# First stage in nine uneven parts, first feed-forward products from unnormalized rows, low-rank products split in two halves of precision, and a new hand-made order

## The chip, the core and the metric

The kernel runs on one core of one Trainium2 chip, as one program with one launch. The metric is the device time of an execution in microseconds (us); less is better. The kernel before has a median of 2166.08 us over three executions (2161.04, 2166.35 and 2166.08). The execution that was profiled took 2172.5 us.

## What is computed

One layer over 256 latent tokens and 256 context tokens of width 2048, all in float32. Cut to what matters here:

```python
mod = silu(c) @ w_ada + b_ada                     # six rows of 2048: shift, scale, gate, twice
h  = modulate(rmsnorm(x, n1), sh1, sc1)           # latent tokens
hc = modulate(rmsnorm(ctx, n1), csh1, csc1)       # context tokens, rows of their own
p  = h @ w_in ; pc = hc @ w_in                    # RWKV r,k,v + low-rank columns, GDN q,k,v, z, gates
# RWKV-7, 16 heads of 64, both directions: decay and in-context rate come from low-rank products,
#   tanh(wd) @ w2 and ad @ a2 (rank 96, two directions each); gate = sigmoid(gd) @ g2
# gated DeltaNet, 8 heads of 128, in chunks, both directions
# final states of the context scans start the latent scans
y  = (sigmoid(g_a) * (o_a @ p_a) + sigmoid(g_b) * (o_b @ p_b)) @ w_out
x  = x + gt1 * y
z  = modulate(rmsnorm(x, n2), sh2, sc2)           # (x * r) * s2 + sh2 with one factor r per token
x  = x + gt2 * (silu(z @ w_gate) * (z @ w_up)) @ w_down
return rmsnorm(x, nf)
```

## The kernel before

**Matrices.** Activations lie with the 2048 channels on 16 tiles of 128 partitions and the tokens on the free axis. Every large product is made in three passes of a faster float32 format (`fp32r`): each operand is cast to a high half `hi` (ScalarE, `whi`) and its remainder `lo` is formed (VectorE, `wlo`), and `gemm` adds hi·hi, hi·lo and lo·hi for each of the 16 tiles of the contraction. A weight tile of 128 columns comes in two pieces of 512 KB over SyncE's DMA queue (`load_w`, or `cast` in the middle stage).

**First stage** (`p0`, lines 440 to 565). x and ctx are loaded, their squares summed, and then eight parts follow, each for two of the 16 channel tiles: four loads of 1 MB of `ada_first`, 64 small TensorE products with it (`ada_part`, line 494), a copy and a transpose (`rows_of`, lines 500 and 502) that make shift and scale, the normalized rows `hxh` and `hxl` (lines 513 to 516), the split of two rows of `w_low` (line 527), and the products of 736 columns that all the rest waits for (`low_products`, through `gemm`, lines 399 to 401): the low-rank columns and the first pair's k and r, in six accumulators. The products of a part stand between the small products of the next one, in amounts that `TILES` sets. At the end two DMAs clear the scratch `tscr` in DRAM from a zero tile of 130 columns.

**Middle stage** (from line 820 on). RWKV pairs, DeltaNet heads, the remaining columns of `w_in` (`products`) and 64 rows of `ada_rest` are written as generators. `Weave` puts their instructions in one order on every engine: it keeps a modelled clock per engine, and picks what could begin first, with `RANK` for ties. This order is what runs (all its instructions show line 147). Tiles of gate columns (`g`), which nothing in this stage needs, fill TensorE; `GATES_A` and `GATES_B` say after which pair or head how many of the 40 become eligible. Products for k, v, K and V cover latent and context tokens at once (512 columns), those for r, Q and g the latent ones (256). The 32 low-rank products (`lowrank`, rank 96) are plain float32.

**After it.** `rows`, the RWKV result, is split into `oah` and `oal` (lines 404 and 405), then come 16 tiles with `p_a`, 16 with `p_b`, 16 with `w_out`. The gate columns are read back (`gate_rows`) into `gts`, which takes the place of `hxh` and `hxl`. During these the last two blocks of `ada_rest` (`scale2`, line 1656) are summed on VectorE, which gives shift and scale of the feed-forward part, and the weights of its first four tiles (`W4`) are loaded and split. Then `rms_scale` (line 418) makes the factor r per token, 16 tiles of `hfh` and `hfl` follow (lines 1753 to 1755), and the first four feed-forward tiles run over them, channel tile by channel tile.

Of the kernel before, what the change touches and what calls it, by code (L numbers as in the profile page):

```python
# [11 lines left out]
F32 = mybir.dt.float32  # L12
# [6 lines left out]
P = 128  # L19
D = 2048  # L20
KT = D // P
# [6 lines left out]
GATES_A, GATES_B = (5, 3, 2, 1, 0, 1, 5, 3), (3, 1, 0, 0, 2, 2, 9, 3)  # L28

RANK = dict(cast=-99, lowrank=194, prepare=47, grams=45, inverse=-73, values=-11, scan=-101, begin=184, head_scan=142, head_inverse=129, head_grams=55, decays=83, outputs=126, head_solve=187, tokens=12, features=125, gate_out=97, lowrank_out=104, row_tile=523)  # L30
# [273 lines left out]
def emit(ctx: ExitStack, tc, A, out, dbg=None):  # L304
# [61 lines left out]
    zero = cst.tile([P, 130], F32, name="zero")  # L366
    G.memset(zero, 0.0)
# [43 lines left out]
    H2 = (hx.tile([P, KT, 2, T], F32R, name="hxh"), hx.tile([P, KT, 2, T], F32R, name="hxl"))  # L411
    HX = tuple(t.rearrange("p k a t -> p k (a t)") for t in H2)
# [27 lines left out]
    NE = 8  # L440
    with tc.tile_pool(name="p0", bufs=1) as p0, \
# [12 lines left out]
        def load_ada(e, c):  # L454
            w = aws[e, c] = p0.tile([P, 4, 4, P], F32, tag="aw", name="aw", bufs=6)
            Q.dma_start(w, A["ada_first"][e, :, 4 * c:4 * c + 4])

        def load_low(e):
            lws[e] = [wp.tile([P, 8, P], F32, tag="wraw", name="wraw", bufs=3).rearrange("p k m -> p (k m)")[:, :NL]
                      for _ in range(2)]  # L460
            for k in range(2):
                Q.dma_start(lws[e][k], A["w_low"][e, :, k])
# [26 lines left out]
        def ada_part(ps, e, c):  # L489

            for i in range(4):
                k = 4 * c + i
                for g in range(4):
                    E.matmul(ps[32 * g:32 * g + 32, 0:P], ckr[:, k].rearrange("p a b -> p (a b)"), aws[e, c][:, i, g],
                             start=k == 0, stop=k == KT - 1)

        def rows_of(e, ps, between):
# [7 lines left out]
            pv = pt[:, 0:P].rearrange("p (a k i) -> p a k i", a=2, k=2)  # L505
            g = slice(2 * e, 2 * e + 2)
            for i, m in enumerate((mod, modc)):
                V.tensor_add(m[:, 0:32].rearrange("p (a k) -> p a k", a=2)[:, :, g], pv[:, :, :, 16 * i],
                             p_("bada")[:, 0:32].rearrange("p (a k) -> p a k", a=2)[:, :, g])
                V.scalar_tensor_tensor(s1[:, i, g], m[:, 16 + 2 * e:18 + 2 * e], 1.0, p_("n1")[:, g], ALU.add, ALU.mult)  # L510
            todo = [(src, i, k, m) for k in range(2 * e, 2 * e + 2) for i, (src, m) in enumerate(((xt, mod), (ct, modc)))]
            for src, i, k, m in todo:
                V.scalar_tensor_tensor(src[:, k, :], src[:, k, :], s1[:, i, k:k + 1], rs[:, i], ALU.mult, ALU.mult)
                S.activation(H2[0][:, k, i, :], src[:, k, :], AF.Identity, bias=m[:, k:k + 1])
            for src, i, k, m in todo:
                V.scalar_tensor_tensor(H2[1][:, k, i, :], src[:, k, :], m[:, k:k + 1], H2[0][:, k, i, :].bitcast(F32),
                                       ALU.add, ALU.subtract)

        def low_split(e):
            res = []  # L520
            for k in range(2):
# [42 lines left out]
        for t in tscr:  # L564
            Q.dma_start(t.rearrange("(p a n) -> p a n", p=P, a=8), zero.unsqueeze(1).to_broadcast([P, 8, 130]))
# [197 lines left out]
    def lowrank():  # L763

        yield s.preload_act_table_set(SIGM)
        lin = rs.tile([P, 2, 8, 2, 64], F32, tag="KBx", name="lin", bufs=2).rearrange("p a b c d -> p (a b c d)")[:96].rearrange("p (j t) -> p j t", j=4)
        raw = rs.tile([P, 4, 64], F32, tag="Y", name="raw").rearrange("p a b -> p (a b)")[:64]
        ab = rs.tile([P, 512], F32, tag="iv0", name="ab")[:32]
        for j, b in ((0, pib), (2, psb), (1, mmb), (3, psb)):
            ps = low[j]  # L770
            yield from shift(ps, 96, 24 + j, lin[:, j])
            if j < 2:
                yield s.activation(lin[:, j], lin[:, j], AF.Tanh)
# [4 lines left out]
            weave.release(b)  # L778
        out = [rs.tile([P, 8, 2, 64], F32, tag=f"VX{i}", name="lo").rearrange("p a b c -> p (a b c)") for i in range(2)]
        out = [t[:, n:n + 512] for t in out for n in (0, 512)]  # L780
        for p in range(NPAIR):
            if p == 2:
# [7 lines left out]
                yield s.activation(sgd, sgd, AF.Exp, scale=-1.0)  # L790
            if p % 2 == 0:
                w = wp.tile([P, 8, P], F32, tag="wraw", name="wraw", bufs=3)
                yield dq(w[:96], A["lora"][p // 2])
            for j in (0, 2, 1, 3):
                ps = yield psb
                yield e.matmul(ps, w[:96, 4 * (p % 2) + j], lin[:, j], start=True, stop=True)
                weave.add(RANK['lowrank_out'], lowrank_out(p, j, ps, out[j]))
# [79 lines left out]
    def grams(p, d):  # L877
# [8 lines left out]
        if d == 0:  # L886
# [33 lines left out]
        p2m, KB, KBx = o["p2m"], o["KB"], o["KBx"]  # L920
# [984 lines left out]
```

## Time and profile before

| what | value |
|---|---|
| median of three executions | 2166.08 us |
| profiled execution: its time, its span | 2172.5 us, 2170.7 us |
| mean granted TensorE clock | 0.988 of full |
| TensorE busy | 2099.3 us, 97% of the span, 24140 matmuls |
| weight loads on TensorE (beside the matmuls) | 1904.9 us, 88% |
| VectorE busy | 1484.0 us, 68% |
| ScalarE busy | 1120.4 us, 52% |
| GpSimd busy | 76.2 us, 4% |
| DMA | 435 MB, 200 GB/s on the mean, 418 GB/s from 25 to 100 us |

PE stands for TensorE's matmuls, PEld for its weight loads, DVE for VectorE, ACT for ScalarE, POOL for GpSimd, SP for SyncE. A row of the timeline gives the start and duration in us, engine, line, operation, output tile, input tiles, shape and count, and in brackets how long the engine was idle before and what it then waited for. A row of the stretches gives for each engine the busy time and the number of instructions, then the granted TensorE clock (PEclk, 1.00 is full), the share of the DMA engines' time and GB/s. Matmuls are pipelined: a duration contains the drain, so the rate is read from one start to the next. A float32 matmul shows as two records.

### The profile page before, as it was taken

Reading aid. Unit: us, or ns where it says so; the run is one execution under the profiler, and the core shown is the slowest. Engines: PE = TensorE matmul, PEld = TensorE weight load, DVE = VectorE, ACT = ScalarE, POOL = GpSimd, SP = SyncE. Lnnn points to the kernel's source line nnn. Section 1 sums busy time; section 2 is a strip of 40 time slices with the busy share of each in tenths; the row PEclk is TensorE's granted clock in tenths of the full one; section 3 lists DMA queues with packets and bytes.
Section 4 is the critical chain, followed back from the end, with each engine's and each line's share of the span. In section 5 each row is a group of like instructions: output and inputs, shape, how many; then the busy total and the mean of one; then the engine's idle time right before and its main releaser. Section 6 shows DMA issues by size and latency. Waiting matters only on the chain.

```text
span 2170.7 us, 56983 instructions
## 1 busy us (share of the span) xinstructions
PE 2099.3 (97%) x24140; PEld 1904.9 (88%) x24140; DVE 1484.0 (68%) x2974; ACT 1120.4 (52%) x2126; POOL 76.2 (4%) x169
## 2 busy tenths in 40 slices
PE   6999999999999999999999999999999999999997
PEld 4777787788888788878988999999999999999997
DVE  4456798888877687898887589856565665444454
ACT  3249853564555666566744555444444444444443
POOL 0000000000000010000010001000000000000000
PEclk9999999999999999999999999999999999999999
DMA  9967544343543364466686899837777775566665
GB/s 387 418 175 204 179 125 116 102 122 102 135 130 103 119 230 131 133 200 186 207 280 216 271 331 342 300 101 234 235 235 231 231 233 192 188 180 186 187 187 156
DMA packets 235278, 435.17 MB, mean 200 GB/s; under 512 B 115216, under 2 KB 130576, under 8 KB 230544
## 3 DMA queue, kind: packets, MB, share of 16 engines
q1 hardware_dynamic: 207376, 356.03, 52.1%
q0 software_dynamic: 13824, 50.34, 7.0%
q10 hardware_dynamic: 13824, 25.17, 3.6%
q8 instruction: 189, 3.10, 0.6%
q14 instruction: 65, 0.53, 0.1%
HBM read 405.63 MB, written 25.84 MB: 199 GB/s over the span
## 4 chain that ended last, share of the span: by engine, by line
issue 51%; PE 9%; DMA 4%; DVE 3%; ACT 1%; POOL 1%; SPq 0%; POOLq 0%; DVEq 0%; ACTq 0%
PE mm L147 6%; DMA aw<-ada_rest 4%; PE pa L147 1%; PE s L147 1%; DVE wlo L147 1%; DVE aw L147 1%; DVE arena L147 1%; PE pi L147 1%; DMA inX<-tscr 0%; POOL aw L1654 0%; DVE inX L147 0%; DMA tscr<-arena 0%; ACT whi L147 0%; POOL aw L125 0%; ACT arena L147 0%
## 5 line engine op out<-in xcount | busy, mean ns | idle before, releaser
L390 DVE TENSOR_TENSOR wlo<-wraw,whi 128x1024 fp32r<-128x1024 f32 x328 | 392.6, 1198 | 325.0 <-ACT whi L389 322.5
L389 ACT CAST whi<-wraw 128x1024 fp32r<-128x1024 f32 x328 | 337.4, 1030 | 464.5 <-PE mm L400 414.6
L147 PE MATMUL mm<-hxh,wlo 128*128 128x256 f32 (+1 forms) x1376 | 463.5, 337 | 7.4 <-DVE wlo L147 7.2
L147 PE MATMUL mm<-hxh,whi 128*128 128x256 f32 (+1 forms) x1376 | 463.2, 337 | 1.7 <-DVE arena L147 1.7
L147 PE MATMUL mm<-hxl,whi 128*128 128x256 f32 (+1 forms) x1376 | 463.4, 337 | 0.6 <-issue 0.6
L400 PE MATMUL mm<-hfl,whi 128*128 128x256 f32 x1344 | 377.3, 281 | 0.0
L401 PE MATMUL mm<-hfh,wlo 128*128 128x256 f32 x1344 | 376.5, 280 | 0.0
L399 PE MATMUL mm<-hfh,whi 128*128 128x256 f32 x1344 | 374.1, 278 | 0.0
L147 PEld LDWEIGHTS mm<-hxh,wlo 128*128 128x128 f32 x1376 | 262.9, 191 | 36.8 <-DVE wlo L147 12.0
L147 DVE TENSOR_TENSOR wlo<-wraw,whi 128x512 fp32r<-128x512 f32 x344 | 234.9, 686 | 79.0 <-ACT whi L147 76.9
L147 PEld LDWEIGHTS mm<-hxh,whi 128*128 128x128 f32 x1376 | 263.1, 191 | 25.2 <-issue 3.1
L147 PEld LDWEIGHTS mm<-hxl,whi 128*128 128x128 f32 x1376 | 263.2, 191 | 25.0 <-issue 4.8
L401 PEld LDWEIGHTS mm<-hfh,wlo 128*128 128x128 f32 x1344 | 252.7, 188 | 0.2
L399 PEld LDWEIGHTS mm<-hfh,whi 128*128 128x128 f32 x1344 | 252.8, 188 | 0.0
L400 PEld LDWEIGHTS mm<-hfl,whi 128*128 128x128 f32 x1344 | 252.4, 188 | 0.0
L147 ACT CAST whi<-wraw 128x512 fp32r<-128x512 f32 x344 | 205.7, 618 | 89.4 <-PE mm L147 74.1
L399 PE MATMUL mm<-za,whi 128*128 128x256 f32 x512 | 143.9, 281 | 0.0
L401 PE MATMUL mm<-za,wlo 128*128 128x256 f32 x512 | 143.8, 281 | 0.0
L400 PE MATMUL mm<-za,whi 128*128 128x256 f32 x512 | 143.7, 281 | 0.0
L401 PEld LDWEIGHTS mm<-za,wlo 128*128 128x128 f32 x512 | 96.6, 189 | 0.0
L399 PEld LDWEIGHTS mm<-za,whi 128*128 128x128 f32 x512 | 96.5, 189 | 0.0
L400 PEld LDWEIGHTS mm<-za,whi 128*128 128x128 f32 x512 | 96.5, 189 | 0.0
(360 smaller groups left out, 3860.6 us busy)
## 6 DMA issues: line engine op xcount, KB each, us to landing
wraw<-w SPq DMA_DIRECT2D x172, 512.0 KB, 3.8
wraw<-wgu SPq DMA_DIRECT2D x168, 512.0 KB, 4.7
aw<-ada_rest POOLq DMA_DIRECT2D x96, 512.0 KB, 5.9
aw<-ada_first SPq DMA_DIRECT2D x32, 1024.0 KB, 13.6
wraw<-wdn SPq DMA_DIRECT2D x64, 448.0 KB, 3.6
wraw<-wout SPq DMA_DIRECT2D x32, 512.0 KB, 6.3
aw<-ada_gt ACTq DMA_DIRECT2D x64, 256.0 KB, 5.0
wraw<-wdn SPq DMA_DIRECT2D x32, 512.0 KB, 3.7
```

What stands on the lines that cost most here:

```text
L147: return Op(self, cost, lambda: getattr(self.engine, name)(out, *a, **k), kind)
L389: S.copy(hi[:, c, :M], raw[:, c, :M])
L390: V.tensor_sub(lo[:, c, :M], raw[:, c, :M], hi[:, c, :M].bitcast(F32))
L399: E.matmul(ps, hi, Xh[:, k, :n], start=first and i == 0, stop=False)
L400: E.matmul(ps, hi, Xl[:, k, :n], start=False, stop=False)
L401: E.matmul(ps, lo, Xh[:, k, :n], start=False, stop=last and i == len(wt) - 1)
```

## The change

**First stage.** Nine parts take the place of eight: one channel tile in the first and in the last, two in the seven between. `ada_first` is laid out for it; a part with one channel tile has two loads of 1 MB instead of four, and its shift and scale are added from two rows of the small products. `TILES` has ten entries. The scratch is no longer cleared here.

**Split tiles.** `hxh` and `hxl` become four tiles, high and low of the latent and of the context tokens (`h00` and so on). Each matmul over 512 columns becomes two over 256 (`parts`), in the order hi·hi latent, hi·hi context, hi·lo latent, hi·lo context, lo·hi latent, lo·hi context.

**Middle stage.** The scratch is cleared in the middle stage by a generator (`zeros`) that fills a tile of 1040 columns on GpSimd and copies it out in two DMAs. Each low-rank product becomes three `fp32r` products; their activations are split after the shift (`lin`), their weights in a generator of its own (`lowrank_weights`), each half of which waits until the previous pair's products have read it (`lowdone`). `RANK`, `GATES_A` and `GATES_B` have new values; several generators wait for one more event, since tiles are shared in another way. `merge_rows` also splits the RWKV result, once the context halves are free (`h01`).

**After it.** `PA` and the gate columns lie in the other three tiles. `scale2` advances by two steps in each of the first ten tiles of `w_out` and one in the eleventh; the four tiles of `W4` are loaded at tiles 10 to 13 and not at 1, 4, 7 and 10. The first four channel tiles of the first four feed-forward tiles are multiplied with x1·s2 without the factor r, together with two columns of the shift (258 columns), before and after `rms_scale`; the result is multiplied by r and added to that of the other twelve channel tiles, which are made as before.

```diff
-GATES_A, GATES_B = (5, 3, 2, 1, 0, 1, 5, 3), (3, 1, 0, 0, 2, 2, 9, 3)
-RANK = dict(cast=-99, lowrank=194, prepare=47, grams=45, inverse=-73, values=-11, scan=-101, begin=184, ...)
+GATES_A, GATES_B = (5, 4, 1, 2, 0, 2, 6, 3), (1, 2, 0, 0, 2, 3, 6, 3)
+RANK = dict(cast=-105, lowrank=22, prepare=69, grams=28, inverse=-48, values=38, scan=-6, begin=131, ...)
...
-    H2 = (hx.tile([P, KT, 2, T], F32R, name="hxh"), hx.tile([P, KT, 2, T], F32R, name="hxl"))
+    H2 = [[hx.tile([P, KT, T], F32R, tag=f"h{i}{j}", name=f"h{i}{j}") for j in range(2)] for i in range(2)]
+    def parts(ps, w, k, n, first, last):
+        hi, lo = w
+        todo = [(u, H2[i][j][:, k], j) for u, i in ((hi, 0), (hi, 1), (lo, 0)) for j in range(n // T)]
+        for i, (u, x, j) in enumerate(todo):
+            yield ps[:, T * j:T * j + T], u, x, first and i == 0, last and i == len(todo) - 1
...
-    NE = 8
+    PARTS = ((0, 1),) + tuple((k, 2) for k in range(1, 15, 2)) + ((15, 1),)
+    NE = len(PARTS)
...
-        TILES = ((0, 0), (2, 2), (2, 2), (2, 2), (1, 3), (2, 2), (1, 3), (1, 2), (2, 2))
+        TILES = ((0, 0), (3, 3), (2, 2), (2, 2), (1, 3), (2, 2), (1, 3), (1, 2), (2, 2), (2, 2))
...
-        for t in tscr:
-            Q.dma_start(t.rearrange("(p a n) -> p a n", p=P, a=8), zero.unsqueeze(1).to_broadcast([P, 8, 130]))
...
+            for i in range(2):
+                yield "lw", p, i
+                hi, lo = lw[i]
+                for j in (i, i + 2):
+                    ps = yield psb
+                    c = slice(P * (j // 2), P * (j // 2) + P)
+                    yield [e.matmul(ps, a[:, c], x, start=n == 0, stop=n == 2)
+                           for n, (a, x) in enumerate(((hi, lin[j][0]), (hi, lin[j][1]), (lo, lin[j][0])))]
+                weave.ready("lowdone", p, i)
...
-            for j in (0, 2, 1, 3):
-                ps = yield psb
-                yield e.matmul(ps, w[:96, 4 * (p % 2) + j], lin[:, j], start=True, stop=True)
+            for i in range(2):                        # lowrank_weights
+                if p:
+                    yield "lowdone", p - 1, i
+                own = w[:96, 4 * (p % 2) + i:4 * (p % 2) + i + 3:2]
+                hi, lo = (t.rearrange("p (j c) -> p j c", j=2) for t in lw[i])
+                yield v.tensor_copy(hi, own)
+                yield v.tensor_sub(lo, own, hi.bitcast(F32))
+                weave.ready("lw", p, i)
...
+        both = hx.tile([P, KT, T], F32R, tag="h01", name="oa")          # merge_rows
+        Oa.extend((both[:, 0:8], both[:, 8:16]))
+        for i in range(0, 8, 2):
+            yield s.copy(Oa[0][:, i:i + 2, :], rows[:, i:i + 2, :])
+            yield v.tensor_sub(Oa[1][:, i:i + 2, :], rows[:, i:i + 2, :], Oa[0][:, i:i + 2, :].bitcast(F32))
...
-        for _ in itertools.islice(scale_next, 2 if j in (0, 3, 6, 9, 12) else 1):
+        for _ in itertools.islice(scale_next, STEPS[j]):                # [2] * 10 + [1] + [0] * 5
...
+    pu = [pst(psq, "s"), pst(psq, "s"), pst(pi, "pi"), pst(pa, "pa")]
+    for a in range(4):
+        gemm(pu[a][:, 0:T + 2], w4[a][:NU], Xu, T + 2)                  # NU = 4
+        if not a:
+            r = rms_scale(x1p, [ssum, sq], T, "rs")
...
-        for k in range(KT):
+        for k in range(NU, KT):
             for a in range(4):
-                gemm(p4[a // 2][:, T * (a % 2):T * (a % 2) + T], w4[a][k:k + 1], Hf, T,
-                     k == 0 and a % 2 == 0, k == KT - 1 and a % 2 == 1)
+                     k == NU and a % 2 == 0, k == KT - 1 and a % 2 == 1)
+        for a in range(4):
+            tc.keep_in_program_order(V.tensor_copy(wsh[:, a:a + 1], pu[a][:, T:T + 1]))
+            tc.keep_in_program_order(V.tensor_mul(both[a // 2][:, T * (a % 2):T * (a % 2) + T], pu[a][:, 0:T], r))
+        for a in range(4):
+            o = slice(T * (a % 2), T * (a % 2) + T)
+            V.scalar_tensor_tensor(both[a // 2][:, o], both[a // 2][:, o], wsh[:, a:a + 1], p4[a // 2][:, o], ALU.add, ALU.add)
```

More of the change, by code (lines that the diff above doesn't have):

```diff
@@ L489, in ada_part @@
         def ada_part(ps, e, c):
[L491 to L495, printed above, removed]
+            n = PARTS[e][1]
+            if (e, c) not in aws:
+                return
+            w = aws[e, c]
+            for i in range(8 // n):
+                k = 8 // n * c + i
+                for a in range(2 * n):
+                    g = 2 * n * (i % (2 // n)) + a
+                    E.matmul(ps[32 * g:32 * g + 32, 0:P], ckr[:, k].rearrange("p a b -> p (a b)"), w[:, i, a],
+                             start=k < 2 // n, stop=k >= KT - 2 // n)
         def rows_of(e, ps, between):
@@ L520, in low_split @@
             res = []
-            for k in range(2):
+            for k in range(PARTS[e][1]):
                 pool = p0 if e % 2 else wp
@@ L770, in lowrank @@
             ps = low[j]
-            yield from shift(ps, 96, 24 + j, lin[:, j])
+            x = full[j % 3 > 0]
+            yield from shift(ps, 96, 24 + j, x)
             if j < 2:
-                yield s.activation(lin[:, j], lin[:, j], AF.Tanh)
+                yield s.activation(x, x, AF.Tanh)
                 yield s.copy(raw[32 * j:32 * j + 32], ps[96:P, 0:T])
@@ L1664, in emit @@
     scale_next = scale2()
[L1665 to L1671 removed]
+    PA = hx.tile([P, KT, T], F32, tag="h11", name="PA")
+    gts = [hx.tile([P, KT, T], F32, tag=f"h{i}0", name=f"gt{i}") for i in range(2)]
     def gate_rows(i):
[L1674 removed]
+        tc.keep_in_program_order(Q.dma_start(gts[i // 4][:, 4 * (i % 4):4 * (i % 4) + 4], gts_[8 + 4 * i:12 + 4 * i].rearrange("j p t -> p j t")))
     gate_rows(0)
@@ new lines, in emit, with scaled @@
+        both = [fp.tile([P, 512], F32, tag="aw", name="both", bufs=3) for _ in range(2)]
+        order, hbs = (*range(NU, KT), *range(NU)), {}
+        def scaled(k):
+            hbs[k] = x1p.tile([P, T], F32, tag="hb", name="hb")
+            V.scalar_tensor_tensor(hbs[k], x1[:, k, :], s2[:, k:k + 1], r, ALU.mult, ALU.mult)
+        scaled(order[0])
+        for n, k in enumerate(order):
+            S.activation(Hf[0][:, k, :], hbs[k], AF.Identity, bias=mod[:, 48 + k:49 + k])
+            if n < KT - 1:
+                scaled(order[n + 1])
+            V.scalar_tensor_tensor(Hf[1][:, k, :], hbs[k], mod[:, 48 + k:49 + k], Hf[0][:, k, :].bitcast(F32),
@@ L1768, in emit @@
             if j < 2:
-                ps = p4[j]
+                ps = both[j]
             else:
```

164 lines of the change are left out of this document (100 added, 64 removed).

## Prediction

> **What bounds the kernel now.** I read the page's busy times first, then stretches of the run, then the gaps on TensorE in the timeline.
>
> ```profile
> PE 2099.3 (97%) x24140; PEld 1904.9 (88%) x24140; DVE 1484.0 (68%) x2974; ACT 1120.4 (52%) x2126; POOL 76.2 (4%) x169
> 50.00:75.00 25.00, 24.91 (x334) 19.77 (x334) 12.18 (x32) 6.29 (x13) 0.00 (x0) 1.00 1.01 418
> 200.00:300.00 100.00, 97.23 (x1453) 75.60 (x1452) 75.00 (x170) 77.17 (x155) 3.58 (x12) 1.00 0.59 167
> 1213.00:1226.00 13.00, 9.88 (x65) 9.22 (x64) 6.53 (x10) 8.02 (x13) 0.00 (x0) 0.87 0.75 250
> 1395.00:1415.00 20.00, 17.93 (x136) 16.66 (x135) 15.98 (x31) 8.10 (x15) 0.00 (x0) 0.91 0.42 147
> 1500.00:1800.00 300.00, 300.00 (x2548) 299.90 (x2547) 179.45 (x264) 127.15 (x160) 0.00 (x0) 1.00 0.73 233
> ```
>
> TensorE bounds all of it (97% busy). In the feed-forward part it is perfect: 2548 matmuls in 300 us, 117.7 ns each at full clock, and nothing of this change touches that. Only in the first stage is DMA equally full (418 GB/s, share 1.01). Two seams are not full: 13 us hold 65 matmuls, which at 117.7 ns are 7.7 us of work, and the clock fell to 0.87; the second has 0.91. So a gain can come from fewer TensorE microseconds, from those seams, or from the head of the first stage; work taken from VectorE (75 of 100 us busy) or ScalarE (77) buys nothing by itself.
>
> **The change part by part.** First, the nine parts.
>
> ```profile
> 24.74 1.08 PE L494 MATMUL mm<-aw,ckr 128*32 128x128 f32 x32 [1.02 <-DMA aw<-ada_first]
> 27.23 1.08 PE L494 MATMUL mm<-aw,ckr 128*32 128x128 f32 x32 [1.40 <-DMA aw<-ada_first]
> 97.01 1.95 PE L494 MATMUL mm<-aw,ckr 128*32 128x128 f32 x64
> 108.95 1.95 PE L494 MATMUL mm<-aw,ckr 128*32 128x128 f32 x64
> 120.81 0.40 PE L399 MATMUL pi<-hxh,whi 128*128 128x512 f32 x1
> 128.48 0.28 PE L147 MATMUL mm<-hxh,whi 128*128 128x256 f32 x1
> 101.04 7.83 SPq L565 DMA_DIRECT2D tscr<-zero  x2
> tscr<-zero SPq DMA_DIRECT2D x2, 520.0 KB, 20.4
> wraw<-w_low SPq DMA_DIRECT2D x16, 368.0 KB, 12.4
> 133.62 0.39 PE L147 MATMUL mm<-hxh,wlo 128*128 128x256 f32 x1 [0.29 <-DVE wlo L147]
> 136.73 0.39 PE L147 MATMUL mm<-hxh,whi 128*128 128x256 f32 x1 [1.67 <-DVE arena L147]
> 137.86 0.39 PE L147 MATMUL mm<-hxh,wlo 128*128 128x256 f32 x1 [0.62 <-DVE wlo L147]
> ```
>
> A load of 1 MB lands every 2.49 us (24.74 to 27.23, TensorE waiting for both), one of `w_low` (0.37 MB) thus in 0.9. A full part costs DMA 4 × 2.49 + 2 × 0.9 = 11.8 us and TensorE 11.94 (97.01 to 108.95): level. Its products are 7.67 us of that (120.81 to 128.48). All bytes and products stay; only the first part's products can begin earlier and the last part's are half as long. Counting landings on from the third megabyte (24.7): the half part's data are there two loads earlier, part 1 is complete at about 34.9, part 2 at 46.7. TensorE, late for neither, ends part 2's turn at 46.7 + 1.0 (last load's small products) + 5.1 (four of six accumulators of part 1) = 52.8, then runs full: five turns × 11.94 = 59.7, and the last: 2.0 + 7.67 + 3.84. That is 126.0 against 128.48: **−2.4 us**. Bounds: 0, if the DMA end holds it, and −5.9, the two loads and one `w_low` that part 0 no longer awaits. Each part adds its small VectorE instructions once more and two more sums in half parts, under 1 us beside TensorE's products.
>
> The scratch: its two DMAs hold SP's queue for 7.83 us and take 20.4 to land, and the middle stage's first weights are issued behind them. TensorE then waits 0.29 and 0.62 us for `wlo`; I take both: **−0.9** (0 if the casts stand behind the shifts anyway). The wait of 1.67 for an accumulator is VectorE's shift; it stays. In the middle stage the fill is one GpSimd instruction on an engine that is 4% busy, and two DMAs of 0.52 MB, about 1.3 us each at 418 GB/s, in SP's queue ahead of a weight load; the share there is 0.59. Cover gone, they delay one cast by 2.6.
>
> Low-rank products, and columns in two halves:
>
> ```profile
> L147 PE MATMUL s<-lin,wraw 96*128 96x512 f32 x64 | 33.1, 618 | 4.1 <-ACT lo L147 4.1
> 155.50 1.89 PE L147 MATMUL s<-lin,wraw 96*128 96x512 f32 x4
> 55.26 0.39 PE L400 MATMUL s<-hxl,whi 128*128 128x512 f32 x1
> 57.35 0.39 PE L400 MATMUL s<-hxl,whi 128*96 128x512 f32 x1
> L147 PE MATMUL mm<-hxl,whi 128*128 128x512 f32 x496 | 206.9, 417 | 0.0
> 176.73 0.69 DVE L147 TENSOR_TENSOR kh<-arena 128x512 f32<-128x512 f32 x1
> 177.33 0.42 DVE L147 TENSOR_TENSOR rin<-arena 128x256 f32<-128x256 f32 x1
> ```
>
> Of four records in 1.89 us the last lasts 0.62 with its drain, so three steps take 1.27: 0.42 each, 0.85 for the two records of one product. Three `fp32r` passes of 512 columns take 3 × 0.232 (nine steps from 55.26 to 57.35 in 2.09) = 0.70. 32 × 0.15 = **−4.8**. Bounds: −9, if the waits of 4.1 us for `lo` go too, and +3, if 96 rows cost a pass more than 128 do. VectorE gets 32 instructions of 256 columns and 8 of 512: 32 × 0.42 + 8 × 0.69 = 19 us at most, between 130 and 250 us, where the row of 200 to 300 leaves it a quarter free; beside TensorE, 0, as long as they are not late (rival below).
>
> Halves: 3 × 496 matmuls in the middle stage and 240 in the first (five accumulators × 16 × 3) of 512 columns become two of 256: 2 × 117.7 − 232 = 3 ns, × 1728 = **+5**. The weight load is repeated, but it lies under the matmul (299.90 of 300 us loading while TensorE keeps 117.7 ns). Bounds: 0, and +10, if 1728 more pairs of instructions make TensorE wait for issue.
>
> The seam ahead of `p_a`:
>
> ```profile
> 1213.35 0.28 PE L147 MATMUL mm<-hxh,wlo 128*128 128x256 f32 x1
> 1215.44 0.50 PE L399 MATMUL mm<-oah,whi 128*128 128x256 f32 x2 [1.81 <-ACT oah L404]
> 1216.51 0.39 PE L400 MATMUL mm<-oal,whi 128*128 128x256 f32 x1 [0.57 <-DVE oal L405]
> 1217.60:1221.00 3.40, 3.40 (x19) 3.40 (x18) 0.66 (x2) 1.09 (x3) 0.00 (x0) 0.50 1.00 342
> 1220.56 0.73 ACT L1684 ACTIVATE gts<-gts 128x256 f32<-128x256 f32 x2 [2.31 <-DMA gts<-gts__1356]
> ```
>
> It loses 1.8 + 0.6 in waits and 1.7 at half clock (3.4 us at 0.50), 5.3 us with smaller waits (13.0 − 7.7). The split of `rows` moves into the middle stage (same instructions, 4 on ScalarE, 4 on VectorE), so the first two waits go and, with them, the fall of the clock. Late next is the gate data: `gts[0]` still lies on tiles that the last gate product reads, and ScalarE, in order, has casts behind that sigmoid. So −4.5, with bounds −1 and −5.3: **−4.5**. `rows` now waits for one event more, and its DMA stands in SP's queue as before.
>
> The first feed-forward products:
>
> ```profile
> 1406.28 0.60 PE L418 MATMUL pa<-arena,C 128*128 128x256 f32 x2
> 1408.95 0.80 PE L399 MATMUL mm<-hfh,w 128*128 128x256 f32 x2 [2.07 <-ACT hfh L1754]
> 1408.70:1412.10 3.40, 3.15 (x14) 3.15 (x15) 2.97 (x9) 1.51 (x4) 0.00 (x0) 0.51 0.29 108
> 1313.00:1345.00 32.00, 32.00 (x275) 31.46 (x274) 30.81 (x40) 18.55 (x22) 3.70 (x7) 1.00 0.97 351
> L390 DVE TENSOR_TENSOR wlo<-wraw,whi 128x1024 fp32r<-128x1024 f32 x32 | 38.6, 1217 | 2.1 <-ACT whi L389 2.1
> L1656 DVE SCALAR_TENSOR_TENSOR acc<-aw,ck,acc 128x1024 f32<-128x1024 f32 x21 | 26.8, 1278 | 0.0
> ```
>
> TensorE waits 2.07 us for r, its logarithm, exponential and the first rows, and then runs 3.4 us at half clock: 3.8 in all, 4.2 with a last sum of `scale2` that no longer stands there. 36 matmuls without r (4.2 us) now stand behind `rms_scale` and cover 2.07; products, 48 of them, are taken from the later ones, 258 columns for 256. **−4.2**, bounds 0 (the new small VectorE work late) and −5. What pays: for ten tiles VectorE has two weight pieces and two `ada_rest` rows per tile, 2 × 1.22 + 2 × 1.28 + 0.9 = 5.9 us against TensorE's 48 × 0.1177 = 5.65. It was 30.81 of 32 before, so this is the old load without its pauses; 2.5 us late in ten tiles, in pieces cast ahead. I take 0, at worst +2.5. The combining of the four tiles comes after, under the next tile's 11.3 us.
>
> The new order I take as 0: it moves gate tiles that have no due time, and TensorE's last work before the seam is gate tiles, so the stage ends when its work is done. This is the largest unknown; the rows of stalls give its size:
>
> ```profile
> 431.42 0.27 PE L147 MATMUL pa<-kh,arena 64*64 64x64 f32 x2 [1.76 <-issue]
> 1117.83 0.24 PE L147 MATMUL pi<-inX,LT 32*32 32x16 f32 x4 [2.04 <-DMA inX<-tscr]
> 1179.06 0.39 PE L147 MATMUL mm<-hxh,wlo 128*128 128x256 f32 x1 [3.24 <-DVE wlo L147]
> 432.50:439.30 6.80, 6.80 (x19) 4.55 (x18) 4.46 (x14) 3.68 (x9) 0.00 (x0) 0.50 0.04 7
> ```
>
> A stall of about 2 us is followed by 3.4 or 6.8 us at clock 0.50, so it costs 4 to 5 in all. These three and 136.73 make some 16 us. A new order may remove nearly all or double them: ±15.
>
> **Sum.** −2.4 − 0.9 − 4.8 + 5 − 4.5 − 4.2 = −11.8, to the profiled execution's 2172.5 us: 2160.7. That execution is 0.3% above the median of 2166.08, and the same share of it gives 2166.08 × 2160.7 / 2172.5 = **2154 us**.
>
> A rule beside this: the Trainium skill, "TensorE: Matmul & The Clock Gate", section "Part 1: The HAM clock gate (the "warmup" mystery)", halves the clock only after an idle window of about 3.4 us. Here waits of 1.8 and 2.07 us were followed by clock 0.50, so the trace disagrees; by the rule the seams would return 3.4 us less.
>
> **The rivals.** (a) The clock falls at the seams as before, for another reason than the wait: then 2 × 1.7 us stay, −8.4, 2158 us. For it: the falls come 1 to 2 us after the wait ended, not in it. Against: 300 us of full work have none. (b) The seams move instead of closing: DMA's end holds the first stage (0), gate data hold the first `p_a` casts (−1), and the sum is −0.9 − 4.8 + 5 − 1 − 4.2 = −5.9, 2160 us, no measurable change (0.3%, some 6.5 us, is what a measurement tells from none); with +2.5 of late VectorE it is 2163. For it: a DMA share of 1.01 in that stage and 2.31 us of wait for `gts`. (c) The new order removes most stalls: −11.8 − 15, 2139. Against: nothing in it is aimed at one. (d) The other side, **slower**: `lowrank_weights`. Each of 16 halves waits until TensorE has read the previous one, then for two VectorE instructions, then TensorE, in order, multiplies: TensorE → VectorE → TensorE. If the order written by a modelled clock is wrong by 1 us at each, TensorE stands 16 us, with the clock halved behind some of them (+5): −11.8 + 21 = +9, 2175. It passes no change at 12 us, 0.75 per half, and counts as slower from 1.15. Against: before, 32 products that waited for ScalarE in the same way lost 4.1 in all.
>
> **How the numbers follow.** Forecast 0.42, (a) 0.08, (b) 0.22, (c) 0.17, (d) 0.11. Faster by over 0.3% are the forecast, (a) and (c): 0.67; the same (b) 0.22; slower (d) 0.11. The range leaves out (d)'s upper half and the far end of (c): 2137 to 2169.
>
> **What would show it.** Last low-rank product of the first stage near 126 us, and no scratch DMA ahead of the first weights; the low-rank products as three passes, 0.70 us a product; 25900 matmuls; no wait for `oah` and a clock of 1.00 in the 13 us after the middle stage; no wait between `rms_scale` and the first rows. Wrong would make it: more stretches at 0.50 in the middle stage than now, or TensorE waiting for split low-rank weights.

## The result and the profile after

The changed kernel took 2154.1 us (median of six executions, 2146.85 to 2156.69) against 2167.24 us for the kernel before (2161.04 to 2170.68). The ratio is 0.9934, 95% interval 0.9917 to 0.9951: by it 14.3 us faster, between 11 and 18 (the two medians are 13.1 apart). The forecast was 2154. The time is right; most of the working that led to it is not, as the experiments show.

The page of the changed kernel, busy time of each engine, and then stretches of its run (start and end in us, then busy time and instructions of TensorE, its weight loads, VectorE, ScalarE and GpSimd, the granted clock, DMA share, GB/s). The first two stretches are the seams, the last two lie in gate and up and in down:

```profile
PE 2070.7 (96%) x25901; PEld 1983.6 (92%) x25901; DVE 1502.0 (70%) x3040; ACT 1127.0 (52%) x2134; POOL 76.5 (4%) x169
1213.00:1226.00 13.00, 11.75 (x98) 11.29 (x97) 5.90 (x10) 7.03 (x12) 0.94 (x2) 1.00 1.02 360
1395.00:1415.00 20.00, 20.00 (x166) 19.89 (x166) 16.67 (x32) 11.74 (x22) 0.00 (x0) 1.00 0.32 109
1500.00:1800.00 300.00, 299.85 (x2566) 299.29 (x2565) 181.42 (x272) 128.27 (x160) 0.00 (x0) 1.00 0.72 232
1940.00:2120.00 180.00, 180.00 (x1576) 180.00 (x1575) 91.17 (x96) 80.18 (x96) 0.00 (x0) 1.00 0.65 192
```

TensorE runs 1761 matmuls more in 28.6 us less of busy time. Both seams hold more work at full clock: 98 matmuls where 65 stood, 166 for 136. The surprise is the last row. Down is untouched by the change, and the same stretch of the kernel before is this:

```profile
1940.00:2120.00 180.00, 180.00 (x1522) 180.00 (x1521) 87.95 (x93) 77.75 (x94) 0.00 (x0) 1.00 0.64 186
```

TensorE was 100% busy at clock 1.00 in both, and yet 1522 matmuls of the same shape became 1576: 118.3 ns each became 114.2. A busy share of 100% and a clock of 1.00 did not mean that the work went at its best rate.

Where the 17.1 us of the two profiled spans came from is read from the starts of a few matmuls. Those of the changed kernel, in the timeline (first small product, first product of the middle stage, last of `p_b`, of `w_out`, of the first four feed-forward tiles, of gate and up, of down):

```profile
23.03 1.96 PE L509 MATMUL mm<-aw,ckr 128*32 128x128 f32 x64
131.72 0.40 PE L147 MATMUL mm<-h,whi 128*128 128x256 f32 x2
1308.98 0.28 PE L399 MATMUL mm<-oa,wlo 128*128 128x256 f32 x1
1402.47 0.28 PE L399 MATMUL mm<-mh,wlo 128*128 128x256 f32 x1
1426.39 0.28 PE L399 MATMUL mm<-hfh,w 128*128 128x256 f32 x1
1898.95 0.28 PE L399 MATMUL mm<-hfh,wlo 128*128 128x256 f32 x1
2141.42 0.28 PE L399 MATMUL mm<-zb,wlo 128*128 128x256 f32 x1
```

The differences of consecutive starts are the second row of this table; every other kernel was read at the same places. The last column is the ratio of its times to those of the kernel before, with its interval.

| kernel | first stage | middle, `p_a`, `p_b` | `w_out` | first 4 tiles | gate, up | down | ratio |
|---|---|---|---|---|---|---|---|
| before | 106.7 | 1184.3 | 91.9 | 29.2 | 474.2 | 250.5 | 1 |
| changed | 108.7 | 1177.3 | 93.5 | 23.9 | 472.6 | 242.5 | 0.9934 (0.9917 to 0.9951) |
| pad32 | 108.3 | 1185.9 | 93.5 | 23.7 | 475.9 | 251.7 | 0.9992 (0.9980 to 1.0004) |
| before_pad32 | 108.1 | 1184.3 | 91.9 | 27.8 | 470.3 | 250.1 | 0.9984 (0.9970 to 0.9998) |
| pad32_both | 108.6 | 1180.0 | 93.5 | 23.6 | 472.3 | 250.1 | 1.0000 (0.9984 to 1.0016) |
| ffn_pad32 | 107.1 | 1177.7 | 93.5 | 23.9 | 475.8 | 242.5 | 0.9957 (0.9940 to 0.9973) |
| before_pad480 | 107.5 | 1174.4 | 91.9 | 29.2 | 470.6 | 242.1 | 0.9935 (0.9915 to 0.9955) |
| ffn_pad160 | 107.3 | 1179.6 | 93.5 | 23.9 | 466.4 | 239.8 | 0.9926 (0.9897 to 0.9956) |
| old_order | 107.7 | 1188.4 | 93.5 | 23.9 | 472.1 | 242.1 | 0.9995 (0.9977 to 1.0013) |
| lowrank_f32 | 108.2 | 1187.1 | 93.5 | 23.9 | 471.8 | 242.5 | 0.9957 (0.9941 to 0.9972) |
| after_placed | 108.5 | 1179.1 | 89.4 | 25.0 | 470.1 | 248.8 | 0.9940 (0.9922 to 0.9958) |
| before_placed | 107.8 | 1177.0 | 90.6 | 28.1 | 474.2 | 248.8 | 0.9955 (0.9935 to 0.9974) |
| halves_alone | 107.5 | 1204.3 | 91.9 | 29.7 | 470.9 | 242.1 | 1.0043 (1.0027 to 1.0059) |
| eight_parts | 108.8 | 1182.5 | 93.5 | 23.9 | 473.2 | 242.5 | 0.9958 (0.9944 to 0.9971) |

A stage is from one profiled execution. Four kernels with the same middle stage (changed, ffn_pad32, ffn_pad160, after_placed) lie between 1177.3 and 1179.6 there, so 2 us in that column mean nothing; their first stages lie between 107.1 and 108.7. The ratios leave out three slow executions of 2848 to 4026 us (one each of ffn_pad32, lowrank_f32 and the kernel before).

### The profile page after: what moved, and what is told of

It is laid out like the page before. It is cut to its first block, busy times and chain, and to the rows that moved or that the text cites. A ratio compares the mean times of both kernels' runs of the same rounds, so it can differ in the third digit from the quotient of the medians.

```text
span 2153.6 us, 60589 instructions
## 1 busy us (share of the span) xinstructions
PE 2070.7 (96%) x25901; PEld 1983.6 (92%) x25901; DVE 1502.0 (70%) x3040; ACT 1127.0 (52%) x2134; POOL 76.5 (4%) x169
## 4 chain that ended last, share of the span: by engine, by line
issue 38%; PE 35%; DVE 11%; DMA 8%; ACT 6%; SPq 1%; POOL 0%; ACTq 0%; POOLq 0%; DVEq 0%
PE mm L147 18%; PE pa L147 5%; DVE arena L147 4%; PE s L147 3%; DVE wlo L147 2%; PE pi L147 2%; DMA aw<-ada_first 2%; PE mm L399 2%; PE mm L398 2%; PE mm L397 2%; ACT arena L147 1%; DVE aw L147 1%; ACT lo L147 1%; ACT whi L147 1%; DMA wraw<-w 1%
## 5 line engine op out<-in xcount | busy, mean ns | idle before, releaser
L147 PE MATMUL mm<-h,whi 128*128 128x256 f32 x3744 | 682.8, 288 | 4.5 <-ACT whi L147 2.7
L147 PEld LDWEIGHTS mm<-h,whi 128*128 128x128 f32 x3744 | 550.9, 190 | 18.0 <-ACT whi L147 4.9
L147 PE MATMUL mm<-h,wlo 128*128 128x256 f32 x1872 | 467.0, 290 | 9.7 <-DVE wlo L147 9.0
L147 PEld LDWEIGHTS mm<-h,wlo 128*128 128x128 f32 x1872 | 322.5, 190 | 20.3 <-DVE wlo L147 14.7
L147 DVE SCALAR_TENSOR_TENSOR aw<-aw,ck 128x512 f32<-128x512 f32 x120 | 88.0, 743 | 7.9 <-DMA aw<-ada_rest 7.8
L399 PE MATMUL mm<-oa,wlo 128*128 128x256 f32 x256 | 71.1, 280 | 2.9 <-DVE wlo L388 2.9
```

What stands on the lines that cost most here:

```text
L147: return Op(self, cost, lambda: getattr(self.engine, name)(out, *a, **k), kind)
L399: E.matmul(ps, lo, Xh[:, k, :n], start=False, stop=last and i == len(wt) - 1)
```

## The experiments

**What differs in down?** Among the edits is the removal of `zero`, 130 columns or 520 bytes a partition behind the constants. All tiles after it moved by 544 bytes: in the compiled kernel the weight pieces start at byte 25120 of a partition, where it was 25664. `za`, `h00` to `h11` and `oa` are laid out from the other end of the memory and stayed. The first theory was that this move, and none of what the change is described as, makes the new rate; the rival, that the order or the chip of the day does.

**pad32**

```diff
     V.memset(scanm.rearrange("p (c t) -> p c t", t=64)[:, :, 0:1], 0.0)
+    pad = cst.tile([P, 8], F32, name="pad")
+    G.memset(pad, 0.0)
```

> The changed kernel with one tile of 32 unused bytes per partition behind the constants, so that all tiles from the weight pieces on lie 32 bytes further: the weight pieces start at 25152, a multiple of 64, as they did before the change (25664), and no longer at 25120. Nothing else differs. Theory (placement): the spacing of the 256-column matmuls, 114.2 ns with p_a, 116.7 with gate and up, 114.5 with down in the changed kernel against 118.4, 117.7 and 118.4 before, comes from where the tiles lie; then it goes back to those values: about +10 us in the middle stage, +3 with p_a, +4 and +7 in the feed-forward part, 2154 + 24 = 2178 us. Rival (the order or the chip of the day): spacing and time stay, 2154 us, within 4.

**before_pad32**: the same two lines in the kernel before.

> The kernel before, with the same 32 unused bytes behind its constants: its weight pieces now start at 25696, 32 beyond a multiple of 64, as in the changed kernel. None of the change's edits is in it. Theory (placement): the spacing falls to that of the changed kernel, about -9 us in the middle stage (4200 products), -3 with p_a, -4 with gate and up and -7 with down: 2167 - 23 = 2144 us, so faster than the changed kernel. Rival: 2167 us, and 118 ns stays.

**pad32_both**: the two lines, and a tile of 32 bytes at the other end, ahead of `hx`.

```diff
+    rp = ent(tc.tile_pool(name="rp", bufs=1, side="right"))
+    G.memset(rp.tile([P, 8], F32, name="rpad"), 0.0)
     hx = hx_ctx.enter_context(tc.tile_pool(name="hx", bufs=1, side="right"))
```

> The changed kernel with 32 unused bytes behind the constants and 32 more at the other end of the memory, where h00 to h11, PA, the gate data and za lie: weight pieces and these tiles all start at multiples of 64, both having been 32 beyond one. Theory A (what counts is how weights and moving rows lie to each other): the middle stage, p_a and down stay at the spacing of the changed kernel (115.0, 114.2, 114.5 ns), gate and up change to 117.7, +4 us: 2158 us. Theory B (the weights' place alone counts): as with the 32 bytes behind the constants alone, near 2178 us. No effect of placement at all: 2154 us.

**ffn_pad32**

```diff
+        G.memset(fp.tile([P, 8], F32, name="fpad"), 0.0)
         zb = fp.tile([P, 2, NH - 32, T], F32R, name="zb")
```

> The changed kernel with 32 unused bytes at the start of the feed-forward part's own tiles, so that zb, hfh and hfl start 32 bytes beyond a multiple of 64, as the weight pieces, za and oa do. Theory (how the two lie to each other counts): gate and up fall from 116.7 to about 113.5 ns a matmul as with za (4032 of them, -13 us), zb's share of down from 116.8 too (576, -2 us): 2139 us. Rival (the weights' place alone, or no effect): 2154 us.

The same stretch of down in pad32, before_pad32 and pad32_both:

```profile
1940.00:2120.00 180.00, 180.00 (x1514) 180.00 (x1513) 87.76 (x93) 77.20 (x93) 0.00 (x0) 1.00 0.63 185
```

```profile
1940.00:2120.00 180.00, 180.00 (x1525) 180.00 (x1524) 87.97 (x92) 76.63 (x91) 0.00 (x0) 1.00 0.64 187
```

```profile
1940.00:2120.00 180.00, 180.00 (x1525) 180.00 (x1524) 87.90 (x92) 77.18 (x92) 0.00 (x0) 1.00 0.64 186
```

32 unused bytes took the whole gain away: pad32, with every edit of the change in it, has ratio 0.9992, and down falls back to 1514 matmuls. So the place of the tiles matters, and the rival of the first run fell, though 2169 us is 9 less than the theory gave. But the rule that I had written, multiples of 64, fell too: before_pad32 gained 0.2% and not 1%, pad32_both was neither of its two theories, and ffn_pad32 made gate and up slower (117.8 ns) instead of faster. What does sort three of the stages is the start of the weight pieces less that of the rows they meet, modulo 512, a weight row of 128 float32: down, `p_a` with `p_b`, and the middle stage are fast where it is 64 (changed, ffn_pad32) and slow where it is 96 (before, pad32) and 128 (before_pad32, pad32_both). In the middle stage this is the distance of nearly all products, in down of the 1536 of 2112 matmuls that read `za`, and in `p_a` and `p_b` of 480 of 768; the others meet `zb` or the second set of weight pieces, at other distances. That reading came after these runs, so it was put to a test of its own: give the unchanged kernel the distance 64.

**before_pad480**: the kernel before, with `pad` of 120 columns in place of 8.

> The kernel before, with 480 unused bytes per partition behind its constants and none of the change's edits. Its weight pieces then start at 26144, so that their distance to the rows they meet (first-stage rows, oah, za) is 64 modulo 512, as in the changed kernel; it was 96 before and 128 with 32 bytes, and neither of those two gained. Theory (the distance modulo 512 sets the spacing, and the change's gain is this alone): middle stage and p_a -7 us, down -8, gate and up between 0 and -3, so 2167 - 16 = 2151 us, the time of the changed kernel. Rival (the gain needs the edits as well): 2167 us.

```profile
1500.00:1800.00 300.00, 300.00 (x2571) 299.81 (x2570) 181.21 (x268) 128.31 (x161) 0.00 (x0) 1.00 0.73 233
1940.00:2120.00 180.00, 180.00 (x1576) 180.00 (x1576) 90.71 (x96) 80.35 (x96) 0.00 (x0) 1.00 0.66 193
```

Ratio 0.9935. An unused tile of 480 bytes, and nothing else, gives the kernel before the time of the changed one; down holds the same 1576 matmuls. Theory confirmed, and by stages about as expected: -9.9 up to the end of `p_b`, -8.4 in down, -3.6 in gate and up. The last of these is not the distance's doing: it is 224 in gate and up in both kernels (see the last section).

**ffn_pad160**: `fpad` of 40 columns, distance 64 for gate and up.

> The changed kernel with 160 unused bytes ahead of the feed-forward part's own tiles: hfh, hfl and zb come to the distance 64 modulo 512 from the weight pieces; it was 224 (116.7 ns a matmul with gate and up), and 192 with 32 bytes (117.8 ns). Theory of the distance: gate and up fall to 113.5 to 114.5 ns as za and oa do, 4032 x 2.7 = -11 us, zb's 576 matmuls -1: 2154 - 12 = 2142 us. Rival (the distance isn't what decides, or not for these tiles): 2154 us.

Gate and up took 466.4 for 472.6, down 239.8: half of what was expected, and the times spread from 2138.89 to 2168.14 us, so the ratio settles little. The trace says why only half. Two stretches of 50 us of the same loop, then TensorE's rows where the one turns into the other:

```profile
1700.00:1750.00 50.00, 50.00 (x427) 50.00 (x426) 30.32 (x47) 21.23 (x26) 0.00 (x0) 1.00 0.71 230
1760.00:1810.00 50.00, 50.00 (x444) 50.00 (x443) 29.32 (x43) 22.40 (x28) 0.00 (x0) 1.00 0.67 220
...
1757.33 0.28 PE L397 MATMUL mm<-hfh,whi 128*128 128x256 f32 x1
1757.45 0.28 PE L398 MATMUL mm<-hfl,whi 128*128 128x256 f32 x1
1757.57 0.33 PE L399 MATMUL mm<-hfh,wlo 128*128 128x256 f32 x1
1757.73 0.28 PE L397 MATMUL mm<-hfh,whi 128*128 128x256 f32 x1
1757.85 0.28 PE L398 MATMUL mm<-hfl,whi 128*128 128x256 f32 x1
1757.96 0.28 PE L399 MATMUL mm<-hfh,wlo 128*128 128x256 f32 x1
```

Up to 1757.57 the steps are 0.12, 0.12; one step of 0.16, and then 0.12, 0.11. The same matmuls on the same tiles have two rates, 117.8 and 113.3 ns, and one step longer by 0.04 us stands where the one turned into the other. In this execution each rate then held from some 45 us to more than 300.

The same run answers whether the weights' own place is what counts: here the weight pieces stayed, only `hfh`, `hfl` and `zb` moved, by 160 bytes, and in down the steps of `zb`'s matmuls fell from 116.8 to 113.3 ns on the mean. In before_pad480 the rows stayed and the weights moved. So neither place alone explains both.

**after_placed**: `fpad` of 40 columns, one of 32 ahead of the second set of weight pieces (`more`), one of 112 ahead of `mh`.

> The changed kernel with all four large products placed: 160 unused bytes ahead of the feed-forward tiles (as in the run with that pad alone, where gate and up with their head of 4 tiles took 6.2 us less and down 2.7 less), and pads of 128 and 448 bytes that bring mh, ml and the second set of weight pieces in w_out to the distance 64 modulo 512; it was 128 and 0 there, at 119.2 ns a matmul. Theory of the distance: w_out falls to 114.5 ns, 768 x 4.7 = -3.6 us, and with the feed-forward part -12.5 us against the changed kernel: 2142 us, a ratio to the kernel before of 0.988. Rival (in w_out VectorE is 97% busy and holds TensorE at 119): -9 us, 0.989 to 0.990.

**before_placed**: the same for the kernel before, 120, 40, 56 and 112 columns.

> The kernel before with 480 unused bytes behind the constants, which alone gave a ratio of 0.9935, and pads that bring hfh, hfl, zb and w_out's tiles to the distance 64 modulo 512 too. None of the change's edits. Theory of the distance: gate and up -5, down -2, w_out -3 us against that run, 2156 - 10 = 2146 us, ratio 0.989; if the edits and their order are worth nothing in sum, the placed changed kernel is equal to it within 3 us. Rival (the edits pay once both are placed): the placed changed kernel is ahead by 5 us or more, since its feed-forward head is 5.3 us shorter.

`w_out` in the changed kernel and then in after_placed:

```profile
1330.00:1390.00 60.00, 60.00 (x509) 58.91 (x508) 55.44 (x67) 29.86 (x38) 6.88 (x13) 1.00 0.96 358
```

```profile
1330.00:1390.00 60.00, 60.00 (x534) 58.92 (x533) 56.26 (x68) 30.36 (x38) 7.25 (x15) 1.00 0.98 363
...
1550.00:1600.00 50.00, 50.00 (x444) 50.00 (x442) 31.53 (x48) 21.83 (x28) 0.00 (x0) 1.00 0.73 240
1610.00:1660.00 50.00, 50.00 (x427) 50.00 (x427) 29.65 (x43) 21.11 (x27) 0.00 (x0) 1.00 0.73 240
1940.00:2120.00 180.00, 180.00 (x1530) 180.00 (x1530) 89.32 (x94) 77.42 (x94) 0.00 (x0) 1.00 0.64 187
```

The distance of 64 did for `w_out` what was expected, -4.1 us, with VectorE as busy as before (55.44 and 56.26 of 60 us), so VectorE was not what held it. But from 1604 us on this execution stayed in the slower of the two rates, up to 2132 us and so through nearly all of down, on the same tiles and addresses on which ffn_pad160 stayed in the faster. Ratios 0.9940 and 0.9955, where 0.988 and 0.989 were expected: placing everything beat neither the changed kernel nor before_pad480. The two placed kernels are equal within their intervals, 3 us apart, so the edits are not seen to pay there either. No version was found that is clearly faster than the changed one.

**The edits.** With the place of the tiles kept as changed, parts of the change were undone.

**old_order**: `RANK`, `GATES_A` and `GATES_B` of the kernel before.

> The changed kernel with the ranks and the numbers of gate tiles of the kernel before, everything else, the tiles' places too, as changed. The prediction took the new order as 0, with 15 us either way as the bound. Theory (the order was fitted to the changed waits and saves stalls that the new work would make): the middle stage is longer by 5 to 15 us, 2159 to 2169. Rival (0): 2154, within 3.

The middle stage is 11.1 us longer, ratio 0.9995: the new order is worth some 13 us, given the other edits. TensorE's waits in the middle stage (engine, line, for whom; us in total, times, longest), of the changed kernel and then of old_order:

```profile
PE mm L147 <- DVE wlo L147: 9.0, 15, 2.0
PE s L147 <- ACT lo L147: 6.7, 8, 1.7
```

```profile
PE mm L147 <- DVE wlo L147: 11.3, 20, 1.7
PE s L147 <- ACT lo L147: 4.8, 5, 2.7
PE s L147 <- DVE VX L147: 4.4, 6, 1.7
PE pa L147 <- ACT y L147: 3.4, 3, 2.2
```

It is no one wait but many small ones, of which these are the largest groups.

**lowrank_f32**

```diff
-                    yield [e.matmul(ps, a[:, c], x, start=n == 0, stop=n == 2)
-                           for n, (a, x) in enumerate(((hi, lin[j][0]), (hi, lin[j][1]), (lo, lin[j][0])))]
+                yield e.matmul(ps, w[:96, 4 * (p % 2) + j], lin[:, j], start=True, stop=True)
...
-        weave.add(RANK['lowrank'] - 10, lowrank_weights(), 0.0)
```

> The changed kernel with its 32 low-rank products in plain float32 again, from unsplit activations and weights: no split of either, 72 VectorE instructions less, the waits of the weights' halves gone. The prediction's term: three passes save 0.15 us a product, so this is 4.8 us slower, 2159 us. Rival, from the spacing in the two traces (64 records took 24.6 us before, 96 take 25.2 after): the split saves nothing on TensorE, and without its VectorE work and its waits this is equal or up to 3 us faster, 2151 to 2154.

It is about 5 us slower (0.9957 against 0.9934; the intervals overlap a little), 9.8 in the profiled middle stage. So the rival's time, equal or faster, is unlikely. But the prediction's reason is not shown by it: in the traces 64 float32 records, start to next start with the waits between, are 24.4 us here and 96 of the other kind 25.2. The difference lies in other waits (`wlo` 9.9 us, 4.8 for issue), under an order that was written for the split products. What the split itself is worth was not separated from that order.

**halves_alone**: the kernel before with the 480 bytes and, of the change, only the halves.

```diff
-                for j, (w, x) in enumerate(((hi, HX[0]), (hi, HX[1]), (lo, HX[0]))):
-                    yield e.matmul(ps[:, :n], w[:, k % 8], x[:, k, :n], start=k + j == 0, stop=k == KT - 1 and j == 2)
+                six = [(w, x[:, k, T * j:T * j + T], j) for w, x in ((hi, HX[0]), (hi, HX[1]), (lo, HX[0])) for j in range(n // T)]
+                for i2, (w, x, j) in enumerate(six):
+                    yield e.matmul(ps[:, T * j:T * j + T], w[:, k % 8], x, start=k + i2 == 0, stop=k == KT - 1 and i2 == len(six) - 1)
...                                                   # and the same in low_products
```

> The kernel before with 480 unused bytes (ratio 0.9935), and of the change only the columns in two halves: each product of 512 columns is made as two of 256 in the same order as in the changed kernel. The prediction's term: +3 ns a pair, 1728 pairs, +5 us: 2161 us. Rival, from the spacing at this placement (232.2 ns for 512 columns, 114.9 for 256): -2.4 ns a pair, -4 us: 2152 us. The written order is made by the same modelled clock and may move the middle stage by several us either way; the spacing of the products tells the two apart then.

Neither: 1204.3 us in the middle stage for 1174.4, ratio 1.0043. The spacing of the halves is about what the rival said (115.2 ns on the mean, counting the steps in which nothing waited; two of them are 2.7 ns less than the 233.2 of one product of 512 columns in before_pad480). Since the halves and the order written from them are all that differs, the rest is most likely the order that the old ranks make of them. The middle stage of this kernel and of before_pad480, and what the clock did:

```profile
135.00:1200.00 1065.00, 1023.05 (x16097) 942.21 (x16098) 829.83 (x2018) 644.50 (x1466) 56.08 (x129) 0.97 0.53 156
```

```profile
135.00:1200.00 1065.00, 1029.44 (x14805) 868.13 (x14804) 843.89 (x2044) 651.11 (x1489) 57.48 (x132) 0.99 0.55 163
```

A mean clock of 0.97 for 0.99 is up to 0.02 x 1065 = 21 us of full rate, the larger part of the 30 us lost: in these stretches the clock was at 0.50 for 55 us and for 14 in before_pad480, and TensorE was idle for 42 us and for 36.

**eight_parts**

```diff
-    PARTS = ((0, 1),) + tuple((k, 2) for k in range(1, 15, 2)) + ((15, 1),)
+    PARTS = tuple((k, 2) for k in range(0, 16, 2))
...
-        TILES = ((0, 0), (3, 3), (2, 2), (2, 2), (1, 3), (2, 2), (1, 3), (1, 2), (2, 2), (2, 2))
+        TILES = ((0, 0), (2, 2), (2, 2), (2, 2), (1, 3), (2, 2), (1, 3), (1, 2), (2, 2))
...                                                   # and ada_first laid out for eight parts
```

> The changed kernel with its first stage in eight equal parts again and the old amounts between them; all else, placement too, as changed. The prediction's term: nine parts end the stage 2.4 us earlier, so this is 2.4 us slower in the stage from the first small product to the first product of the middle stage (108.7 us in the changed kernel, 107.1 to 108.6 in its variants): about 110.5. Rival, from the traces (TensorE has the same 95 us of work behind the same late loads in both): no gain, 106.7 to 108.1 as in the three runs of the kernel before and its variants, 0 to -1.5 us.

The first stage takes 108.8 us for 108.7: nine parts gain nothing there, and the rival holds. Yet the kernel is about 5 us slower (0.9958; the intervals overlap a little). Some 2 us of that stand right behind the stage, where the middle stage begins: 91 matmuls in its first 20 us, where the changed kernel has 110. Two variants with the first stage and the order as changed, pad32 and ffn_pad32, reach the hundredth matmul of the middle stage within 0.2 us of the changed kernel, eight_parts 2.0 us behind it. The rest comes later in the middle stage, where kernels with the same middle stage differ as much. First eight_parts, then the changed kernel:

```profile
130.05 0.50 PE L147 MATMUL mm<-h,whi 128*128 128x256 f32 x2 [1.28 <-ACT whi L147]
132.96 0.58 PE L147 MATMUL mm<-h,wlo 128*128 128x256 f32 x1 [2.41 <-DVE wlo L147]
...
130.05:150.05 20.00, 15.55 (x91) 14.32 (x92) 17.97 (x43) 9.88 (x17) 0.00 (x0) 0.74 0.28 90
131.20:138.00 6.80, 5.04 (x21) 4.71 (x22) 4.84 (x12) 5.09 (x8) 0.00 (x0) 0.50 0.14 34
```

```profile
132.90 0.39 PE L147 MATMUL mm<-h,wlo 128*128 128x256 f32 x1 [0.78 <-DVE wlo L147]
135.21 0.50 PE L147 MATMUL mm<-h,whi 128*128 128x256 f32 x2 [0.89 <-ACT whi L147]
142.78 0.50 PE L147 MATMUL mm<-h,whi 128*128 128x256 f32 x2 [1.76 <-ACT whi L147]
...
131.72:151.72 20.00, 15.14 (x110) 13.13 (x109) 17.31 (x42) 11.08 (x20) 0.00 (x0) 1.00 0.34 114
```

TensorE waits 3.7 us for the first weights to be cast, likely since ScalarE and VectorE have a full last part ahead of them, and the clock is 0.74 on the mean of those 20 us. By the Trainium skill, "TensorE: Matmul & The Clock Gate", section "Part 1: The HAM clock gate (the "warmup" mystery)", the clock is halved after an idle window of about 3.4 us. Here it fell to 0.50 at 131.2 us, behind a wait of 1.28 us and 0.7 us into one of 2.41; two waits of 0.89 and 1.76 us, 7.6 us apart, left it at 1.00 in the changed kernel.

## Why the prediction was right, and where it was not

The time was right, and "faster" was right, by luck: two errors cancel, 13 us from the places of the tiles that were not in the sum, and 12 us of edits in the sum that are not there. The step that failed is the very first choice: that every part of this change is an instruction, a wait or an order. The removal of 520 bytes was costed as a transfer saved in SP's queue; that it moves the weight pieces was not seen, and the sentence "nothing of this change touches that" about the feed-forward part is wrong (250.5 to 242.5 us in down). Of its signs, the 25901 matmuls, the loads ahead of the scratch and the two seams came; the end of the first stage near 126 us (131.7) and 0.70 us for three low-rank passes (0.79) did not. Term by term:

- **Nine parts, -2.4**: measured about 0 (eight_parts 108.8, changed 108.7). The turn of part 2 ended where it was put (53.42 us, for 52.8 and a start 1.3 us later). The sum of the last turn failed: it left out the two accumulators of the part before that were still to do. The rows:

```profile
113.68 0.27 PE L517 MATMUL pa<-C,rows 128*128 128x128 f32 x1
117.41 1.95 PE L509 MATMUL mm<-aw,ckr 128*32 128x128 f32 x64
119.29 0.72 PE L556 MATMUL pi<-h,whi 128*128 128x256 f32 x4
127.16 1.30 PE L556 MATMUL pi<-h,whi 128*128 128x256 f32 x4
```

  From the last full turn's end, 113.68, come 3.7 us of the old part, 1.9 of small products, 7.9 and 4.5 of products, up to the middle stage's first at 131.72: 18.0 and not 13.5. If the nine parts gain anything, it is the 2 us behind the stage, at the start of the middle stage, where the prediction did not look.
- **Scratch, -0.9**: 0. The waits for `wlo` at the start of the middle stage are still there (0.78), and two for `whi` of 0.89 and 1.76 beside them: the first casts were late, not the loads.
- **Low-rank, -4.8**: the group of 64 records, 33.1 us busy with 4.1 of waits, became this:

```profile
L147 PE MATMUL s<-lin,lw 96*128 96x512 f32 x96 | 27.2, 405 | 6.7 <-ACT lo L147 6.7
```

  TensorE's busy time fell by 5.9, but its wait for ScalarE's `lo` grew by 2.6, and start to start the group is 25.2 us for 24.6: nothing. Both prices were mis-sized: float32 takes 24.6 / 32 = 0.77 us a product, not the 0.85 that one row gave, and three passes take 25.2 / 32 = 0.79, not 0.70.
- **Halves, +5**: the sign depends on the place. By the mean of the steps in which nothing waited, two halves are 236.2 ns (2 x 118.1 in pad32) against 233.8 for one product of 512 columns at the distance 96, and 230.5 (halves_alone) against 233.2 (before_pad480) at 64: +3.6 or -4.0 us for the 1488 pairs of the middle stage.
- **Seam ahead of `p_a`, -4.5**: right at the place (no wait for `oah`, clock 1.00, 33 matmuls more in 13 us, which is 3.8 us). TensorE's waits from 1226 to 1312 us are 3.0 us in all, where they were 1.8, the longest for a cast of weights; whether these 1.2 us are a part of the seam come back, as rival (b) has it, is not shown:

```profile
1284.62 0.39 PE L399 MATMUL mm<-oa,wlo 128*128 128x256 f32 x1 [1.42 <-DVE wlo L388]
```

- **First feed-forward products, -4.2, with VectorE's load in `w_out`, 0**: the head went from 29.2 to 23.9 us, a little beyond the bound of -5, and `w_out` from 91.9 to 93.5. Together that is -3.7, and -4.3 between the two placed kernels (118.7 to 114.4): right. The 1.6 us in `w_out` are not VectorE's, since after_placed has the same VectorE work there and 89.4.
- **New order, 0**: wrong by 13 us, inside its bound of 15. It is not a gain over the kernel before, as rival (c) had it: it wins back what the other edits cost under the old ranks (old_order is as slow as the kernel before, and halves_alone is 23 us slower than before_pad480).

So at one and the same distance in the middle stage, `p_a`, `p_b` and down, the edits with their order are worth nothing: 0.9992 against 1 at 96, 0.9934 against 0.9935 at 64. What the seam and the halves gain is lost elsewhere in the middle stage: with `p_a` and `p_b` it is 2.9 us longer in the changed kernel than in before_pad480, and TensorE is idle there from 135 to 1200 us for 41.9 us, where it is 35.6 in before_pad480:

```profile
135.00:1200.00 1065.00, 1023.13 (x16300) 957.32 (x16300) 855.93 (x2081) 655.56 (x1491) 55.27 (x129) 0.99 0.54 160
```

Which edit makes these waits was not separated. Rival (d), that the weights' halves stall TensorE, did not come. Rival (a) is out: the clock is 1.00 in both seams.

## What to carry to other kernels

Before an edit is credited, compare a stretch that it does not touch, by matmuls per microsecond and not by busy share; if that moved, ask whether the tiles did, and a pad of a few bytes in either kernel, timed over many executions, tells the edit from the move. When a hand-made order was fitted to a kernel, an edit under the old order and one under a new order are two experiments: here 13 us lay between them. Count the last turn of a pipeline piece by piece, and look for its gain in the first waits of the next stage.

## What was not expected of the hardware

The rate of TensorE, fully busy at clock 1.00, depends on where weights and moving rows lie to each other: 1576 matmuls of 256 columns in 180 us at the distance 64 modulo 512, 1514 to 1525 at 96 and 128. The Trainium skill, "TensorE: Matmul & The Clock Gate", section "Back-to-back issue gap", gives N / 2.4 + 2.5 ns for the gap of a single matmul, by which 109 ns would be the estimate for 256 columns, and says that in a stream the weight loads help to set it. No stretch of this shape here kept to 109, and the traces show several rates for it, 113.3, 114.2, 116.7, 117.8 and more.

Beside that, one loop on fixed tiles has two rates, and one longer step stands at the changes that were read closely, longer by 0.04 us in ffn_pad160 and by 0.2 in after_placed. At the distance 64 the rates are 113.3 and 117.8 ns (444 and 427 matmuls in 50 us), and one held from 28 us (before_placed, 1590 to 1618 us) to some 520 us (after_placed). At 224 they are 116.7 and 117.8: gate and up kept 116.7 ns nearly throughout in seven kernels, but in the kernel before only up to 1507 us, in eight_parts only from 1598 us on, and in pad32 only from 1676 to 1765 us. Two stretches of pad32:

```profile
1690.00:1740.00 50.00, 50.00 (x430) 49.97 (x430) 30.16 (x46) 20.87 (x26) 0.00 (x0) 1.00 0.74 238
1790.00:1840.00 50.00, 50.00 (x427) 50.00 (x426) 27.54 (x38) 20.90 (x26) 0.00 (x0) 1.00 0.59 192
```

So the 2 to 4 us by which gate and up differ between kernels with the distance 224 are the rate that an execution happened to be in, and the 117.8 ns of ffn_pad32 at 192 may be the slower of two as well. In down, the executions at 96 and 128 kept 118.1 ns or more, and no faster rate was seen there. That the two rates are what spreads the times of one kernel (2138.89 to 2168.14 for ffn_pad160) is likely, but only argued: one execution of each was profiled. Why the distance matters, whether 512 is the right modulus, and what picks the rate after a longer step, stays open.
